# Transposes of v, decayed keys, outputs and weights moved from TensorE to VectorE's 32x32 squares and DRAM, in both mixers of a streaming encoder step

## The chip, the cores and the metric

One Trainium2 chip, one of its cores. The metric is device time in microseconds (us) of one launch, the median of three runs. TensorE (PE) does matrix products, VectorE (DVE) and ScalarE (ACT) elementwise work, GpSimd (POOL) a few small operations, SyncE (SP) issues nearly all DMAs.

## The reference, cut to what matters

One step of a two-layer encoder, on 256 prompt frames of a new stream and 32 frames of a running one, model width 1024, hidden width 2816:

```python
for l in range(2):
    x = x + 0.5 * swiglu(rms(x), ffn1)            # (silu(h @ w_gate) * (h @ w_up)) @ w_down
    x = x + (mixer_ab if l == 0 else mixer_c)(rms(x))
    x = x + 0.5 * swiglu(rms(x), ffn2)

def mixer_ab(h):                                   # 8 heads of 128 in A, 8 heads of 128 in B
    q, f, v, g, bq, bk, bv = split(h @ w_in)
    f = lb + (1 - lb) * sigmoid(f)
    # A: S_t = diag(f_t) S_{t-1} + (1 - f_t) v_t^T ;  o_t = S_t^T silu(q_t)
    o_a = rms(o) * g_out * sigmoid(g)
    # B: A[t,s] = sigmoid(z_ts) * prod_{s<j<t} (1 - sigmoid(z_tj)),  z = rms(bq) . rms(bk)
    return concat(o_a, A @ bv) @ w_out             # also returned: S, the normed bk, bv

def mixer_c(h):
    u, v = split(gelu(h @ w_in)); v = layernorm(v)
    return (u * (w_s @ v + b_s)) @ w_out           # w_s: 8 groups of 128 x 128, over positions
```

## The kernel before

Activations lie transposed, channels on the 128 partitions and 288 frames along them (32 sample frames, then 256 of the prompt). Every weight matrix is cut into chunks, of mostly 1024 rows by 256 columns, in the order in which they are used (the list `stream`). A chunk is fetched by one DMA on SP's queue, three chunks ahead (`next_chunk`, tile `wraw`), and split into a high part on ACT (`wh`, line 220) and the rest on DVE (`wl`, line 221). Each block of 128 x 128 then costs three products of 288 columns, lines 260 to 262, with the input's own two parts: 48 for a chunk of eight block rows. These are called the mains below. Two PSUM pairs named `acc` take the results of chunks in turn, four single buffers take everything else.

Mixer A/B handles the heads in four pairs. For each pair seven chunks run, f, q, v, g, bv, bk and bq (`GROUPS`). DVE's evacuation (lines 317, 318) scales each result by the norm's reciprocal. When v is there, the generator `hgrn` starts: it transposes v through DRAM (`to_rows`: DVE transposes 32 x 32 squares, four DMAs on SP put the squares in their places, one DMA reads the rows back as `vt`), runs seven levels of decay products (lines 596 to 617: A, Z, the QK rows, E and f), each with a score product on PE (line 623) whose result DVE puts in place (COPY_PREDICATED, line 633), then transposes the decayed keys on PE (line 142, `kt<-tmp`), makes the state S (696) and the outputs o (712 to 718), normalises them on ACT by squares (720), a power on POOL and a scaled copy (731), transposes them back on PE (158 and 160, `oT`) and gates them. For B, `stick_keys` and `stick` normalise bk and bq, make the stick-breaking weights (833 to 867), transpose them on PE (872 `wTs`, 883 `wT`) and multiply by values (891 to 901, `ob`). Mixer C runs eight chunks of v and eight of u, transposes each v on PE (988, `vt`), takes means of it (997), and after the eighth v normalises all of it (1038) and mixes positions (1063, 1082, `sp`). The last norm's blocks leave through `result`: six by DVE's squares and SP, two by PE transposes `y` (1330).

The generators stand in lanes: `tick`, after each block row of a chunk, gives every lane credit by its rate, and a lane with one credit takes a step to its next `yield`. The rates of the two A/B lanes are RATES, that of mixer C's is C_RATE. This is the order in which the code is written. A scheduler then settles the order on each engine, and within one engine the instructions run in that settled order, each when its semaphores allow.

Of the kernel before, what the change touches and what calls it, by code (L numbers as in the profile page):

```python
# [93 lines left out]
class Net:  # L94
    PIECE = 2
    NORM_RATE = 0.17
    RATES = (0.65, 0.55)

    def __init__(self, tc, ctx, I, O):
# [8 lines left out]
        self.rows = e(tc.tile_pool(name="rows", bufs=2, space=bass.MemoryType.DRAM))  # L108
# [287 lines left out]
    def resid(self, j, b, acc, scale, gnext):  # L396
# [4 lines left out]
        if scale == 1.0:  # L401
            nc.vector.tensor_tensor(out=x, in0=acc[b][:, :NT], in1=x, op=ALU.add)  # L402
        else:
            nc.vector.scalar_tensor_tensor(out=x, in0=acc[b][:, :NT], scalar=scale, in1=x,  # L404
                                           op0=ALU.mult, op1=ALU.add)
# [128 lines left out]
    def hgrn(self, p, pool, d):  # L534
# [146 lines left out]
        kts = []  # L681
        for b in range(2):
# [3 lines left out]
            if b == 0:  # L686
                for h in range(2):
                    r = slice(TS * h, TS * h + TS)
                    nc.scalar.copy(out=ktz[r, h], in_=pk[r, TP:TP + P])
            kts.append(kt)  # L690
            yield
        for b in range(2):
            kt = kts[b]
            pn = self.ps("S")
            for w, (x, y) in enumerate(((kt[:, 0], vw(b)[:, 0]), (kt[:, 1], vw(b)[:, 1]), (ktz[:, b], vs))):
# [9 lines left out]
        g = d["g"]  # L705
        nc.scalar.activation(out=g, in_=g, func=AF.Sigmoid)
# [20 lines left out]
        yield  # L727
        for b in range(2):
            on = T("on", [P, 384])
            for w in range(3 - b):  # L730
                nc.scalar.activation(out=on[:, w * P:w * P + P], in_=po[b][:, w * P:w * P + P], func=AF.Copy,
                                     scale=rs[:, 3 * b + w:3 * b + w + 1])
            yield
            pt = self.to_cols("oT", b, on[:, :TP].rearrange("p (w c) -> p w c", c=P), on[:, TP:])
            parts = [(b, slice(TS, NT), pt[:, :TP])]
            if b == 0:
# [645 lines left out]
```

## Time and profile before

| | us |
|---|---|
| median of 3 runs (1324.56 to 1324.66) | 1324.58 |
| the profiled execution | 1324.58 |
| its span in the trace | 1322.9 |
| PE busy | 1317.1 (100%) |
| DVE busy | 887.1 (67%) |
| ACT busy | 661.7 (50%) |
| POOL busy | 41.7 (3%) |
| DMA of the busiest queue, share of 16 engines | 53.5% |

Busy means that an instruction of the engine was at work. Matmuls overlap their neighbours in the pipeline, so what one costs is read from start to start, not from its own duration. Between the span and the profiled execution's time lie 1.7 us at the two ends. Mixer A/B runs from 260 to about 500 us of the span, each of its first three whole pairs in 61.3 to 61.4 us; mixer C from 940 to 1065 us.

### The profile page before, as it was taken

What the parts mean: (1) busy time and instruction counts of PE and PEld (TensorE: products, weight loads), DVE (VectorE), ACT (ScalarE), POOL (GpSimd) and SP (SyncE); (2) the same over time, 40 slices, a digit from 0 to 9 for tenths busy, and PEclk for the clock granted to TensorE, in tenths of its full rate; (3) what the DMA queues carried; (4) which work ended last, traced back from release to release, by engine and by line L of the source; (5) the groups of instructions that cost most, each with busy time, mean ns of one, the idle gap of its engine ahead of it and who ended that gap; (6) DMA issues with size and microseconds to landing.
All of it is one profiled execution on the core that took longest, in us unless ns stands there. A gap on an engine that the chain in (4) does not pass through costs nothing.

```text
span 1322.9 us, 24562 instructions
## 1 busy us (share of the span) xinstructions
PE 1317.1 (100%) x9922; PEld 1310.3 (99%) x9922; DVE 887.1 (67%) x1706; ACT 661.7 (50%) x1355; POOL 41.7 (3%) x70
## 2 busy tenths in 40 slices
PE   9999999999999999999999999999999999999998
PEld 9999999999999999999999999999999999999998
DVE  7666556889898866666655756655567976666653
ACT  7544445464746465544444644444655446444432
POOL 1000000010101000000000000030000000000000
PEclk9999999999999999999999999999999999999999
DMA  9555455565565546555545555576544545555453
GB/s 283 178 176 168 150 175 173 157 182 159 168 170 170 140 134 200 161 178 166 157 153 174 165 179 165 161 183 188 169 152 138 167 147 160 173 166 171 152 152 84
DMA packets 254852, 219.83 MB, mean 166 GB/s; under 512 B 41233, under 2 KB 254018, under 8 KB 254738
## 3 DMA queue, kind: packets, MB, share of 16 engines
q1 hardware_dynamic: 253906, 216.32, 53.5%
q0 software_dynamic: 672, 1.77, 0.7%
q8 instruction: 78, 1.28, 0.4%
q10 hardware_dynamic: 160, 0.17, 0.1%
q14 instruction: 36, 0.29, 0.1%
HBM read 210.89 MB, written 7.34 MB: 165 GB/s over the span
## 4 chain that ended last, share of the span: by engine, by line
PE 97%; DVE 2%; ACT 0%; issue 0%; POOL 0%; DVEq 0%
PE acc L262 30%; PE acc L261 30%; PE acc L260 30%; PE sc L623 1%; DVE wl L221 1%; PE sp L1082 1%; PE S L696 0%; PE zs L833 0%; PE acc L1157 0%; PE sc L651 0%; PE ob L900 0%; PE vt L988 0%; PE acc L280 0%; PE z L845 0%; PE ob L895 0%
## 5 line engine op out<-in xcount | busy, mean ns | idle before, releaser
L220 ACT CAST wh<-wraw 128x512 fp32r<-128x512 f32 x768 | 440.5, 619 | 490.3 <-PE acc L262 370.1
L221 DVE TENSOR_TENSOR wl<-wraw,wh 128x512 fp32r<-128x512 f32 x768 | 507.4, 688 | 253.4 <-ACT wh L220 252.9
L260 PE MATMUL acc<-xh,wl 128*128 128x288 f32 x2096 | 627.2, 299 | 0.0
L261 PE MATMUL acc<-xl,wh 128*128 128x288 f32 x2096 | 619.4, 295 | 0.0
L262 PE MATMUL acc<-xh,wh 128*128 128x288 f32 x2096 | 618.9, 295 | 0.0
L261 PEld LDWEIGHTS acc<-xl,wh 128*128 128x128 f32 x2096 | 394.1, 188 | 0.6
L260 PEld LDWEIGHTS acc<-xh,wl 128*128 128x128 f32 x2096 | 393.9, 188 | 0.4
L262 PEld LDWEIGHTS acc<-xh,wh 128*128 128x128 f32 x2096 | 393.6, 188 | 0.2
L260 PE MATMUL acc<-hh,wl 128*128 128x288 f32 x960 | 284.5, 297 | 0.0
L261 PE MATMUL acc<-hl,wh 128*128 128x288 f32 x960 | 283.4, 295 | 0.0
L262 PE MATMUL acc<-hh,wh 128*128 128x288 f32 x960 | 282.8, 295 | 0.0
L260 PEld LDWEIGHTS acc<-hh,wl 128*128 128x128 f32 x960 | 180.2, 188 | 0.8 <-DVE xT L402 0.2
L261 PEld LDWEIGHTS acc<-hl,wh 128*128 128x128 f32 x960 | 180.3, 188 | 0.1
L262 PEld LDWEIGHTS acc<-hh,wh 128*128 128x128 f32 x960 | 180.3, 188 | 0.0
L309 DVE TENSOR_TENSOR u<-acc,rb 128x576 f32<-128x576 f32 x52 | 39.3, 757 | 48.8 <-PE acc L262 48.8
L309 DVE TENSOR_TENSOR g<-acc,rb 128x576 f32<-128x576 f32 x47 | 35.6, 757 | 47.0 <-PE acc L262 47.0
L329 ACT CAST hh<-u 128x576 fp32r<-128x576 f32 x52 | 35.1, 675 | 58.4 <-DVE u L455 40.3
L330 DVE TENSOR_TENSOR hl<-u,hh 128x576 fp32r<-128x576 f32 x52 | 39.4, 758 | 7.1 <-ACT hh L329 1.3
L336 ACT ACTIVATE xh<-xT,cols 128x288 fp32r<-128x288 f32 x40 | 21.2, 531 | 24.8 <-DVE xT L404 15.4
L455 DVE TENSOR_TENSOR u<-u,g 128x576 f32<-128x576 f32 x44 | 33.1, 752 | 0.0
L453 ACT ACTIVATE g<-g 128x576 f32<-128x576 f32 x44 | 30.0, 682 | 0.1
L404 DVE SCALAR_TENSOR_TENSOR xT<-acc,xT 128x288 f32<-128x288 f32 x32 | 14.5, 455 | 17.0 <-PE acc L262 17.0
(303 smaller groups left out, 759.1 us busy)
## 6 DMA issues: line engine op xcount, KB each, us to landing
wraw<-in_ffn_w_up_dram SPq DMA_DIRECT2D x44, 1024.0 KB, 5.9
wraw<-in_ffn_w_gate_dram SPq DMA_DIRECT2D x43, 1024.0 KB, 5.4
wraw<-in_ffn_w_down_dram SPq DMA_DIRECT2D x32, 1024.0 KB, 5.7
wraw<-in_ab_w_in_dram SPq DMA_DIRECT2D x28, 1024.0 KB, 5.0
wraw<-in_c_w_in_dram SPq DMA_DIRECT2D x16, 1024.0 KB, 5.5
wraw<-in_ffn_w_down_dram SPq DMA_DIRECT2D x16, 768.0 KB, 4.6
wraw<-in_c_w_out_dram SPq DMA_DIRECT2D x8, 1024.0 KB, 5.6
wraw<-in_ab_w_out_dram SPq DMA_DIRECT2D x8, 768.0 KB, 5.2
```

Source lines behind the costliest of these rows:

```text
L220: self.nc.scalar.copy(out=h[:, x], in_=w[:, a:b])
L221: self.nc.vector.tensor_tensor(out=l[:, x], in0=w[:, a:b], in1=h[:, x].bitcast(F32), op=ALU.subtract)
L260: mm(o, lhsT=l[:, k, c], rhs=hi[:, r], start=st, stop=False)
L261: mm(o, lhsT=h[:, k, c], rhs=lo[:, r], start=False, stop=False)
L262: mm(o, lhsT=h[:, k, c], rhs=hi[:, r], start=False, stop=en)
L309: self.nc.vector.tensor_tensor(out=x, in0=acc[:, :, :NT], in1=self.rb, op=ALU.mult)
L329: nc.scalar.copy(out=hh, in_=h)
L330: nc.vector.tensor_tensor(out=self.hl[:, k:k + 2], in0=h, in1=hh.bitcast(F32), op=ALU.subtract)
L336: nc.scalar.activation(out=self.xh[:, k], in_=x, func=AF.Copy, scale=g)
L404: nc.vector.scalar_tensor_tensor(out=x, in0=acc[b][:, :NT], scalar=scale, in1=x, op0=ALU.mult, op1=ALU.add)
L453: nc.scalar.activation(out=g, in_=g, func=AF.Silu)
L455: nc.vector.tensor_tensor(out=u, in0=u, in1=g, op=ALU.mult)
```

## The change

In mixer A/B, per pair of heads: `kt` and `ktz` (decayed keys), four of the five output transposes and the two `wT` groups no longer come from PE. DVE transposes 32 x 32 squares into a tile, four DMAs on SP write them to a DRAM row tile, and one DMA (for `ktz` two more) reads them back. Seven empty steps stand between a transfer and its use. The four scalings of f by the lower bounds move from DVE to ACT. The sigmoid of g moves ahead of S. RATES go from 0.65 and 0.55 to 0.85 and 0.62, and the DRAM row tiles from 2 buffers to 6. In mixer C each v is transposed the same way in a lane of its own with rate 1.0, and means are taken one step later. The first norm's means and squares of a row stand one step ahead of its splits. At the end block 6 leaves by DVE's squares, four of its DMAs from ACT's queue, and block 7 is added up in two halves and leaves by three DMAs. Line numbers after the change are some 2 to 9 higher.

```diff
-    RATES = (0.65, 0.55)
+    RATES = (0.85, 0.62)
-        self.rows = e(tc.tile_pool(name="rows", bufs=2, space=bass.MemoryType.DRAM))
+        self.rows = e(tc.tile_pool(name="rows", bufs=6, space=bass.MemoryType.DRAM))
...
+            cuts = (0, TS + P, NT) if gnext is None and k == KD - 1 else (0, NT)
+            for a, e in zip(cuts, cuts[1:]):
+                nc.vector.scalar_tensor_tensor(out=x[:, a:e], in0=acc[b][:, a:e], scalar=scale, in1=x[:, a:e],
+                                               op0=ALU.mult, op1=ALU.add)
...
-                nc.vector.tensor_scalar(out=x, in0=x, scalar1=self.lbc[:, h:h + 1],
-                                        scalar2=self.lb[:, h:h + 1], op0=mul, op1=ALU.add)
+                nc.scalar.activation(out=x, in_=x, func=AF.Identity, scale=self.lbc[:, h:h + 1],
+                                     bias=self.lb[:, h:h + 1])
...
-            pk = self.to_tok(kd, b, "kt")
-            kt = T("kt", [P, 2, P], 2)
-            nc.scalar.copy(out=kt, in_=pk[:, :TP].rearrange("p (w c) -> p w c", c=P))
...
+        kt = T("kt", [P, 4, P])
+        rows = self.to_rows(T("QK", [P, S2 + N2], 2)[:, 0:N2], [(0, kd)])
+        nc.sync.dma_start(out=kt, in_=rows[S2:].rearrange("(i t) c -> t i c", t=P))
+        for h in range(2):
+            r = slice(TS * h, TS * h + TS)
+            nc.sync.dma_start(out=ktz[r, h], in_=rows[r])
+        g = d["g"]
+        nc.scalar.activation(out=g, in_=g, func=AF.Sigmoid)
+        for _ in range(7):
+            yield
...
-            pt = self.to_cols("oT", b, on[:, :TP].rearrange("p (w c) -> p w c", c=P), on[:, TP:])
...
+        nc.scalar.activation(out=os, in_=po[0][:, TP:384], func=AF.Copy, scale=rs[:, 2:3])
+        rows = self.to_rows(T("QK", [P, S2 + N2], 2)[:, 0:4 * P], [(0, on)])
+        ot = T("vt", [P, 5, P])
+        nc.sync.dma_start(out=ot[:, 0:4], in_=rows.rearrange("(i c) t -> c i t", c=P))
+        yield
+        pt = self.ps("oT")
+        nc.tensor.transpose(pt[:, 0:P], os, self.ident)
...
+        for _ in range(7):
+            yield
+        for h in range(2):
+            gated(h, slice(TS, NT), ot[:, 2 * h:2 * h + 2].rearrange("p w t -> p (w t)"))
...
-                nc.tensor.transpose(pw[:, i * P:i * P + P], B[b][:, i * P:i * P + P], self.ident)
...
+        for b in range(2):
+            wT = T(("wT", "pk")[b], ([P, 384], [P, 2, PAST])[b])
+            wT = wT if b == 0 else wT.rearrange("p h s -> p (h s)")[:, 0:384]
+            rows = self.to_rows(y[:, 384 * b:384 * b + 384], [(0, B[b])])
+            nc.sync.dma_start(out=wT.rearrange("p (i t) -> p i t", t=P), in_=rows.rearrange("(i s) t -> s i t", s=P))
...
-            lane = Lane(self.C_RATE)
-            self.lanes = [lane]
+            fast, lane = self.lanes = [Lane(1.0), Lane(self.C_RATE)]
...
-                        nc.tensor.transpose(pv[:, a:a + P], v[:, b, s:e], self.ident)
-                nc.scalar.copy(out=vt[:, :, n * 256:n * 256 + 256], in_=pv.rearrange("p (w c) -> p w c", w=2))
+                rows = self.to_rows(y, [(TP * b, v[:, b, TS:]) for b in range(2)])
+                for b in range(2):
+                    c = n * 256 + b * P
+                    nc.sync.dma_start(out=vt[:, :, c:c + P],
+                                      in_=rows[TP * b:TP * b + TP].rearrange("(w t) c -> t w c", t=P))
...
+            nc.vector.bn_stats(part[:n, w], xs[w][:n, 0:512])
+            nc.scalar.activation(out=junk[:n], in_=xs[w][:n, 512:D], func=AF.Square, scale=D ** -0.5,
+                                 accum_out=sa[:n, w:w + 1])
             next(split)
...
-        if k < KD - 2:
+        if k < KD - 1:
...
+                eng = nc.scalar if k == KD - 2 and a == 0 else nc.sync
...
+        for w, copy in ((0, nc.scalar.copy), (2, nc.vector.tensor_copy), (1, nc.vector.tensor_copy)):
+            n, c = ROWS[w], slice(w * P, w * P + P)
+            copy(out=y[:n, c], in_=po[:n, c])
+            to = O[1][0, :, cs] if w == 2 else O[0][0, w * P:w * P + P, cs]
+            (nc.scalar if w == 2 else nc.sync).dma_start(out=to, in_=y[:n, c])
```

What stands in a row on an engine, at three places. The first is TensorE around the score products of a middle pair of heads in mixer A/B. Before, `sc` are the scores of successive levels, and acc_4492 and acc_4587 the pair's bv and bk chunks:

```order
L262 MATMUL acc_4492<-xh,wh_4440 128x288
L623 MATMUL sc_4581<-QK_4524 128x128 x2
L260 MATMUL acc_4587<-xh,wl_4502 128x288
...
L262 MATMUL acc_4587<-xh,wh_4501 128x288
L623 MATMUL sc_4622<-QK_4558 128x128 x2
L626 MATMUL sc_4622<-QK_4558 128x128
L260 MATMUL acc_4587<-xh,wl_4502 128x288
...
L262 MATMUL acc_4587<-xh,wh_4542 128x288
L623 MATMUL sc_4657<-QK_4602 128x128 x2
L628 MATMUL sc_4657<-QK_4602 128x64
L260 MATMUL acc_4587<-xh,wl_4543 128x288
```

Before, 18 mains stand between one score and the next. After, with acc_4719 the pair's bq chunk and acc_4844 the next pair's f chunk:

```order
L262 MATMUL acc_4719<-xh,wh_4682 128x288
L625 MATMUL sc_4531<-QK_4474 128x128 x2
L628 MATMUL sc_4531<-QK_4474 128x128
L909 MATMUL ob_4535<-pk_4335,bvt_3937 128x256
L625 MATMUL sc_4565<-QK_4514 128x128 x2
L625 MATMUL sc_4600<-QK_4550 128x128 x2
...
L625 MATMUL sc_4661<-QK_4612 128x128 x2
L625 MATMUL sc_4692<-QK_4647 128x128 x2
L142 MATMUL kt_4792<-ident,bk_4716 128x128 x2
L144 MATMUL kt_4792<-ident,bk_4716 128x128
L142 MATMUL kt_4809<-ident,bk_4716 128x128 x2
L260 MATMUL acc_4844<-xh,wl_4729 128x288
```

After, six scores, an `ob` product and the three groups that transpose bk (`kt<-ident,bk`) follow each other with no main between them; the first main behind them reads wl_4729.

The second place is VectorE over the same stretch. Before, `bq_4813` is the evacuation of the bq chunk (acc_4686); wl_4696 and wl_4771 are the two halves of the next pair's f chunk, wl_4826 the first half of its q chunk:

```order
L221 TENSOR_TENSOR wl_4696<-wraw_4493,wh_4695 128x512
...
L221 TENSOR_TENSOR wl_4771<-wraw_4493,wh_4770 128x512
L617 TENSOR_TENSOR f_4141<-f_4141 128x4x64
L221 TENSOR_TENSOR wl_4771<-wraw_4493,wh_4770 128x512
L673 TENSOR_TENSOR qz_2519<-q_4261,f_4141 128x2x32
L674 TENSOR_TENSOR q_4261<-q_4261,f_4141 128x256
L676 TENSOR_TENSOR tmp_4797<-k_4391,E_4398 128x320
L677 TENSOR_TENSOR tmp_4797<-k_4391,E_4398 128x2x128
L781 TENSOR_SCALAR ks_4756<-kms_4755 128x5
L221 TENSOR_TENSOR wl_4826<-wraw_4588,wh_4825 128x512
L317 TENSOR_TENSOR bq_4813<-acc_4686,rb_2579 128x2x2x128
```

Before, all of the f chunk's splits stand ahead of the evacuation. After, `bq_4841` is the evacuation, and wl_4729 the first half of the next pair's f chunk:

```order
L221 TENSOR_TENSOR wl_4683<-wraw_4386,wh_4682 128x512 x2
...
L618 TENSOR_TENSOR E_4418<-E_4418,f_4170 128x144x2
L317 TENSOR_TENSOR bq_4841<-acc_4719,rb_2579 128x2x2x128
L619 TENSOR_TENSOR f_4170<-f_4170 128x144x2
L598 TENSOR_TENSOR QK_4514<-k_4411,E_4418 128x40x4
...
L635 COPY_PREDICATED sc_4443<-lv,sc_4531 128x128x2
...
L676 TENSOR_TENSOR q_4276<-q_4276,f_4170 128x256
L679 TENSOR_TENSOR tmp_4713<-k_4411,E_4418 128x2x128
L221 TENSOR_TENSOR wl_4729<-wraw_4500,wh_4728 128x512
L168 STREAM_TRANSPOSE QK_4735<-tmp_4713 128x576
L221 TENSOR_TENSOR wl_4729<-wraw_4500,wh_4728 128x512
```

After, 41 rows of the levels and their end (left out in part) stand between the evacuation of bq and the first split for the next chunk; before, the levels' end stood ahead of the evacuation.

The third place is VectorE in mixer C, where v gives way to u. Before, wl_11528 and wl_11569 are the halves of the second u chunk (acc_11612), and v_11437 and v_11514 the evacuations of the last two v chunks:

```order
L221 TENSOR_TENSOR wl_11485<-wraw_11291,wh_11484 128x512 x2
L221 TENSOR_TENSOR wl_11528<-wraw_11367,wh_11527 128x512 x2
L309 TENSOR_TENSOR v_11437<-acc_11366,rb_10949 128x576
L221 TENSOR_TENSOR wl_11569<-wraw_11367,wh_11568 128x512 x2
L309 TENSOR_TENSOR v_11514<-acc_11441,rb_10949 128x576
L997 BN_STATS st_10885<-vt_10882 128x6 x2
```

After, u_11667 and u_11770 are the evacuations of the first and second u chunk (acc_11591, acc_11681); wl_11601 and wl_11644 are the halves of the second, wl_11691 the first half of the third (acc_11773):

```order
L168 STREAM_TRANSPOSE lnb_11525<-v_11508 128x256 x2
L309 TENSOR_TENSOR u_11667<-acc_11591,rb_10977 128x576
L221 TENSOR_TENSOR wl_11601<-wraw_11433,wh_11600 128x512 x2
L221 TENSOR_TENSOR wl_11644<-wraw_11433,wh_11643 128x512 x2
L168 STREAM_TRANSPOSE vo_11604<-v_11587 128x256 x2
L309 TENSOR_TENSOR u_11770<-acc_11681,rb_10977 128x576
L221 TENSOR_TENSOR wl_11691<-wraw_11513,wh_11690 128x512
```

Before, a chunk's first split stood ahead of the evacuations of the chunks that run two and three places before it. After, it stands right behind the evacuation of the chunk that runs just before it.

## Rows read from the trace of the kernel before

**Rows 1.** The page: busy times, granted clock in 40 slices, chain of waits.

```profile
PE 1317.1 (100%) x9922; PEld 1310.3 (99%) x9922; DVE 887.1 (67%) x1706; ACT 661.7 (50%) x1355; POOL 41.7 (3%) x70
...
PEclk9999999999999999999999999999999999999999
...
PE 97%; DVE 2%; ACT 0%; issue 0%; POOL 0%; DVEq 0%
```

**Rows 2.** TensorE's waits: total us, times, longest; the five there are, first and last.

```profile
PE acc L1157 <- DVE ms L1168: 1.2, 1, 1.2
...
PE kn L158 <- DVE bkt L786: 0.2, 1, 0.2
```

**Rows 3.** Windows: window, length, busy us (instructions) PE, PEld, DVE, ACT, POOL, clock, DMA.

```profile
24.00:200.00 176.00, 176.00 (x1330) 176.00 (x1329) 109.64 (x181) 84.03 (x146) 0.00 (x0) 1.00 0.55 173
```

**Rows 4.** Timeline of TensorE, three key transposes between mains: start us, length us.

```profile
334.22 0.30 PE L262 MATMUL acc<-xh,wh 128*128 128x288 f32 x1
334.35 0.38 PE L142 MATMUL kt<-ident,tmp 128*128 128x128 f32 x2
...
334.82 0.30 PE L261 MATMUL acc<-xl,wh 128*128 128x288 f32 x1
```

**Rows 5.** Timeline of VectorE, one level of decay products with its placement.

```profile
376.03 0.32 DVE L596 TENSOR_TENSOR QK<-k,E 128x160 f32<-128x160 f32 x1
376.26 0.29 DVE L597 TENSOR_TENSOR QK<-k,E 128x128 f32<-128x128 f32 x1
...
377.27 0.73 DVE L633 COPY_PREDICATED sc<-lv,sc 128x256 f32<-128x256 uint8 x1
377.79 0.50 DVE L617 TENSOR_TENSOR f<-f 128x288 f32<-128x288 f32 x1
378.20 0.32 DVE L596 TENSOR_TENSOR QK<-k,E 128x160 f32<-128x160 f32 x1
```

**Rows 6.** Groups of VectorE, 306.27 to 490.30 us: busy us, mean ns, idle before.

```profile
L221 DVE TENSOR_TENSOR wl<-wraw,wh 128x512 fp32r<-128x512 f32 x83 | 55.5, 688 | 5.7 <-ACT wh L220 5.4
L639 DVE COPY_PREDICATED SS<-ls,sc 64x64 f32<-64x64 uint8 x15 | 3.4, 224 | 0.1
L168 DVE STREAM_TRANSPOSE kn<-bv 128x576 f32<-128x576 f32 x3 | 2.3, 762 | 0.0
L317 DVE TENSOR_TENSOR bq<-acc,rb 128x512 f32<-128x512 f32 x3 | 2.0, 678 | 0.0
```

**Rows 7.** Timeline of TensorE, one score (three products in it) between mains.

```profile
375.77 0.30 PE L262 MATMUL acc<-xh,wh 128*128 128x288 f32 x1
375.91 0.61 PE L623 MATMUL sc<-QK 128*128 128x128 f32 x4
...
376.71 0.30 PE L261 MATMUL acc<-xl,wh 128*128 128x288 f32 x1
```

**Rows 8.** Groups of ScalarE and GpSimd, 306.27 to 490.30 us, in the normalisation.

```profile
L731 ACT ACTIVATE on<-o,pw 128x128 f32<-128x128 f32 x15 | 4.6, 374 | 0.1
...
L720 ACT ACTIVATE on<-o 128x128 f32<-128x128 f32 x15 | 4.1, 275 | 7.7 <-PE o L718 6.8 <-PE o L714 0.6
...
L720 ACT ACTIVATION_READ_ACCUMULATOR on<-o 128x1 f32 x15 | 2.9, 194 | 0.0
...
L134 POOL TENSOR_TENSOR pw<-oms,mhalf 128x5 f32<-128x5 f32 x3 | 3.8, 1256 | 34.0 <-DVE oms L724 34.0
```

**Rows 9.** A window of mixer C, where positions are mixed; columns as in rows 3.

```profile
1020.00:1030.00 10.00, 10.00 (x80) 10.00 (x80) 10.00 (x23) 4.84 (x9) 0.00 (x0) 1.00 0.44 126
```

**Rows 10.** DMA issues: queue, operation, count, KB of each, median us to landing.

```profile
rows<-QK SPq DMA_DIRECT2D x16, 80.0 KB, 2.1
vt<-rows SPq DMA_DIRECT2D x4, 320.0 KB, 4.6
```

**Rows 11.** Timeline of the end: the last sum and the last copy before the output.

```profile
1318.37 0.46 DVE L404 SCALAR_TENSOR_TENSOR xT<-acc,xT 128x288 f32<-128x288 f32 x1 [1.95 <-PE acc L262]
...
1319.46 0.37 ACT L1332 COPY sq<-y 128x256 f32<-128x256 f32 x1 [0.40 <-PE y L1330]
```

More of the change, by code (lines that the diff above doesn't have):

```diff
@@ L680, in hgrn @@
         Sn = T("Sn", [P, 2, 2, P])
-        kts = []
-        for b in range(2):
-            pk = self.to_tok(kd, b, "kt")
-            kt = T("kt", [P, 2, P], 2)
-            nc.scalar.copy(out=kt, in_=pk[:, :TP].rearrange("p (w c) -> p w c", c=P))
[L686 to L690, printed above, removed]
+        kt = T("kt", [P, 4, P])
[7 more added lines that the diff above has]
+        for _ in range(7):
             yield
         for b in range(2):
-            kt = kts[b]
             pn = self.ps("S")
-            for w, (x, y) in enumerate(((kt[:, 0], vw(b)[:, 0]), (kt[:, 1], vw(b)[:, 1]), (ktz[:, b], vs))):
+            for w, (x, y) in enumerate(((kt[:, b], vw(b)[:, 0]), (kt[:, 2 + b], vw(b)[:, 1]), (ktz[:, b], vs))):
                 mm(pn[:, w * P:w * P + P], lhsT=x, rhs=y, start=True, stop=True)
@@ L878, in store @@
             nc.vector.tensor_tensor(out=self.hl[:, k, t], in0=x, in1=self.hh[:, k, t].bitcast(F32), op=ALU.subtract)
-        def turned(b):
-            pw = self.ps("wT")
-            for i in range(3):
-                nc.tensor.transpose(pw[:, i * P:i * P + P], B[b][:, i * P:i * P + P], self.ident)
-            wT = T("wT", [P, 384])
-            nc.scalar.copy(out=wT, in_=pw[:, :384])
-            return wT
-        wT = turned(0)
+        wTs = []
+        y = T("kn", [P, 2 * (PAST + NT)])
+        for b in range(2):
[3 more added lines that the diff above has]
+            nc.sync.dma_start(out=wT.rearrange("p (i t) -> p i t", t=P), in_=rows.rearrange("(i s) t -> s i t", s=P))
+            wTs.append(wT)
         yield
@@ L896, in stick @@
         store(slice(kk, kk + 2), slice(0, TS), po[:, 0:S2].rearrange("p (h t) -> p h t", h=2))
-        yield
+        for _ in range(7):
+            yield
         for b in range(2):
             po = self.ps("ob")
+            wT = wTs[b]
             mm(po[:, 0:256], lhsT=vt[:, 1 + b], rhs=wT[:, 0:256], start=True, stop=False)
             mm(po[:, 128:256], lhsT=vt[:, 3 + b], rhs=wT[:, 256:384], start=False, stop=True)
-            if b == 0:
-                wT = turned(1)
             store(kk + b, slice(TS, NT), po[:, :TP])
@@ L995, in tokens @@
                     nc.scalar.copy(out=vs[:, j], in_=pv[:, :P])
-                    for w in range(2):
-                        nc.vector.bn_stats(st[:, w, j], vt[:, w, (n - 1) * 256:(n + 1) * 256])
-                    yield
+                elif n:
+                    means(n // 2 - 1)
+                yield
             spw = spatial_weights()
@@ L1018, in statistics @@
                 mv = state["mv"] = T("mv", [P, 3, 2])
+                means(J - 1)
                 sp = T("sp", [P, 6])
@@ L1042, in sample_out @@
             def sample_out():
[L1044 removed]
+                gb, bb, y = (T(n, [P, J * P]).rearrange("p (j c) -> p j c", c=P) for n in ("lng", "lnb", "vo"))
                 for to, name in ((gb, "c_ln_g"), (bb, "c_ln_b")):
@@ L1239, in first_block @@
                 keep(5, a)
-            nc.vector.bn_stats(part[:n, w], xs[w][:n, 0:512])
-            nc.scalar.activation(out=junk[:n], in_=xs[w][:n, 512:D], func=AF.Square, scale=D ** -0.5,
-                                 accum_out=sa[:n, w:w + 1])
         for w, n in enumerate(ROWS):
```

50 lines of the change are left out of this document (18 added, 32 removed).

## The prediction

> **What bounds the kernel now.** I read the page first. TensorE is busy for 1317.1 of the span's 1322.9 us and makes 97% of the chain of waits [rows 1]; VectorE is busy for 67% and ScalarE for 50%. The view of TensorE's waits sums to 2.3 us in five waits [rows 2]. So the time is TensorE's own instructions in a row, and an edit gains what it takes from that row and loses what it makes TensorE wait. In a window of nothing but mains, 1330 of them take 176.00 us, 0.132 us each [rows 3]. Then I read the order of the changed kernel against that of before, and asked at each place what TensorE has at hand when a row of the other engines becomes serial. Durations below are rows of before.
>
> **What TensorE is rid of.** Per pair of heads 5 transposes of keys, 4 of outputs and 6 of weights go, in four pairs 60; in mixer C 32 and at the end 3: 95 together. Three of them between two mains move the main after next from 334.22 + 0.27 to 334.82 [rows 4]: 0.60 - 0.27 = 0.33, so 0.11 us each. 95 x 0.11 = **-10.4 us**. The copies of their results on ScalarE, the scalings moved to it and the 32 x 32 transposes on VectorE (0.76 us for 576 columns [rows 6]) lie beside mains as long as TensorE has any; both engines have room, and I cost them at nothing outside the places below. A rule of the Trainium skill speaks against this part: "VectorE: DVE Perf Modes", "Rules for kernel authors", leaves a full 128 x 128 transpose to TensorE where the result may lie in PSUM, and the 32 x 32 ones to VectorE. By it this term would be 0; the rows, with TensorE full, price it at -10.4, and I take the rows.
>
> **The score bunches.** This is the largest term. Before, a score product stands between each 18 mains, and the next pair's f chunk is split on VectorE before bq is evacuated. After, in pairs 1, 2 and 3 (pair 0 keeps its spacing), six scores stand together behind the bq chunk, and VectorE has evacuation, 41 rows, and only then the first split on which the next main waits. The evacuation needs the last main of bq, so none of it can run ahead. Summed: evacuation 0.68 [rows 6]; four levels with placement at 378.20 - 376.03 = 2.17 [rows 5], 8.7; the last level without placement and sample columns, 2.17 - 0.52 - 0.2, 1.5; the first f 0.4; four placements of the sample at 0.22, 0.9 [rows 6]; the part of `hl` and the closing products qz, tmp twice and q, five of some 0.2 to 0.5, between a small and a large row of [rows 6], 1.6; the split 0.69 [rows 6]. That is 14.5; rows that follow each other overlap by some 0.1 (0.32 long, next start 0.23 later [rows 5]), where the levels' 2.17 holds this already, so I take 13.8. TensorE has in that time the scores: one with three products costs 376.71 - 375.77 - 0.27 = 0.67 [rows 7], with two of them two thirds, 0.44; three of each, 3.3. Five transposes of bk are 0.55, the `ob` product by columns (384 against 128 at 0.22) 0.7 to 0.9: 4.8. So 13.8 - 4.8 = 9.0 idle per bunch, x 3 = **+27 us**. Bounds: the levels at their rate without overlap 14.5, at a tenth less 12.4, which gives 23 to 29.
>
> **The smaller waits per pair.** From one pair's S bunch to the next score bunch I find six, three times over.
> (1) bk to bq: the evacuation and then the split of bq stand behind the last main of bk: 0.68 + 0.69 [rows 6], 1.4.
> (2) The transposes `ss` of bq take the PSUM buffer that the scaled copies (731 before) release. Behind the last o product come two squares at 0.275 + 0.194, POOL's power 1.26 and four copies at 0.374 [rows 8], with VectorE's small step 0.2 in between: 3.9 + 0.3 for the hand-overs, against 18 mains, 2.4: 1.8.
> (3) The one `oT` transpose left waits for its scaled copy, which stands on ScalarE behind three copies of kn, bq's scaling, a sigmoid, five squares and a cast: 26 mains cover 3.4 of some 5: 1.5.
> (4) `wTs` waits for the sample's scan on VectorE: 1.0. (5) Its product waits for ScalarE's copy behind eight sigmoids: 0.4.
> (6) The bv chunk's first split stands behind the placement of a score that closes the chunk before: 0.52 [rows 5] and 0.69, 1.2.
> Sum 7.3, x 3 = **+21.9**. I have (3) to (5) from rows of ScalarE and VectorE alone and take 0 and double as their ends; (1), (2) and (6) to within a third: 3 x (3 to 11.7), 9 to 35.
>
> **The end of mixer A/B.** The last pair has the same waits with less cover: `ss` 1.9, `oT` with 3 mains instead of 26 ahead of it 4.6, `wTs` 0.7. Then two `ob` products wait for the weights' way through DRAM: a write lands 2.1 after its issue, a read of rows up to 4.6 [rows 10], against some 6 us of mains and products that stand between: 3. The output chunk waits for the last `hl`, 1. **+11**, between 5 (reads of this size at 2.1) and 15.
>
> **Mixer C.** There the first split of five chunks (the first to fifth of u) now stands right behind the evacuation of the chunk ahead: 0.76 - 0.1 + 0.69 = 1.4 each, with some 0.6 for second halves behind means: 7.6. The normalisation of v comes two chunks later than before. VectorE is busy there for all of ten us [rows 9], while TensorE lives on splits made ahead. After, that lead is gone: behind the evacuation of the fourth u chunk TensorE waits for POOL's power and the first normalised columns (2.3), and the sixth's first split stands behind the rest of the normalisation and one spatial step, nine scalings of 0.46 and some 4.6 of products, 9.4 with the split, while TensorE has 5 us: 4.4. Together **+14**, between 5, if half of the splits are early enough after all, and 20.
>
> **The ends.** The norm's step at the start: TensorE is fed by the weights there, 0 within 0.5. At the end the last sum of 0.46 goes in two halves and the copy of 0.37 likewise [rows 11]; a half of each leaves the path, **-0.4**, within 0.5.
>
> Sum: 1324.6 - 10.4 + 27 + 21.9 + 11 + 14 - 0.4 = 1387.7, against the profiled execution, which is the median of the runs (its span plus 1.7 us). I forecast **1388 us**, +4.8%.
>
> **The rivals.**
> The transposes alone: VectorE's row is done while TensorE has work, and 1324.6 - 10.8 = 1314 stands. For it: VectorE is only 67% busy. Its place is the score bunch, and it decides when all waits together fall under 10.8 us, 3.6 per bunch with none elsewhere, that is when the row behind bq's evacuation takes 8.4 us instead of 13.8. Against it: the level's 2.17 us are a plain row of VectorE's work without a wait in it [rows 5].
> Only the score bunches: the smaller waits and mixer C are covered, since every idle time of TensorE lets the others get ahead. 1324.6 - 10.8 + 27 = 1341. For it: those waits are each under 2 us and read from several engines' rows.
> TensorE's clock: it is granted in full in all 40 slices of before [rows 1], where TensorE never rests. In a bunch it is at work for a third of 14 us. If the clock falls there to the lower of its two levels, 1.2 of 2.4 GHz, the mains behind it take twice as long until it is back. No row of before shows how long that would be. Between nothing and one chunk, 48 x 0.132 = 6.4 us, I take 3.2 at five places (three bunches, the end of A/B, the sixth u chunk): +16, 1404. The Trainium skill has this rule, in "TensorE: Matmul & The Clock Gate", section "Part 1: The HAM clock gate": an idle array is throttled to 1.2 GHz and is given its full rate after sustained work. No row of before can show it.
> DRAM's way: the keys' or outputs' read lands after TensorE asks for it in every pair, since four writes and three reads stand on SP's queue among weight fetches. Twice 2.1 + 4.6 [rows 10] against the 60 and more mains (8 us) that stand between write and S would cost some 3 to 5 us a pair: 1400.
> That nothing is changed in effect (within 0.2%, about what a measurement of this kernel can tell) would need waits of 8 to 13 us in all.
>
> **How the numbers follow.** Forecast 0.50, clock 0.19, only the bunches 0.13, DRAM's way 0.07, transposes alone 0.09, no difference 0.02. Faster is 0.09, same 0.02, slower 0.89. The range leaves out the transposes alone and a little above the clock's case: from 1338, the bunches alone with their lower bound, to 1408.
>
> **What would show it.** In the profile after, TensorE's busy share falls to about 95%, and its waits name VectorE's split (line 221) in first place with three waits of about 9 us, at one place per pair, then ScalarE's scaled copy and line 221 again in mixer C. VectorE and ScalarE grow by little. A granted clock under 1.00 behind a bunch would show the third rival, waits on reads of rows the fourth. The prediction is wrong if the view of TensorE's waits sums to less than 20 us, or if its largest waits lie elsewhere.

## The result

The changed kernel takes 1406.62 us in the median (1403.83 to 1408.56), the kernel before 1324.57 in the same comparison: 1.0618 times as long, 95% interval 1.0599 to 1.0637. The profiled execution takes 1407.47 us with a span of 1405.8, so 82.9 us more than the 1324.58 of before. The forecast was 1388 us, with a range of 1338 to 1408.

The page of the changed kernel, its lines that answer to [rows 1]:

```profile
PE 1339.5 (95%) x9827; PEld 1321.9 (94%) x9827; DVE 897.7 (64%) x1724; ACT 655.1 (47%) x1338; POOL 45.1 (3%) x70
...
PEclk9999999998998988999999999999998899999999
...
PE 86%; DVE 7%; issue 4%; ACT 2%; POOL 1%; DMA 0%; POOLq 0%; ACTq 0%; DVEq 0%
```

95 of TensorE's instructions are gone, and yet it is busy for 22.4 us longer: the clock has holes, and a product takes longer in them. TensorE's waits, which were five and 2.3 us together [rows 2], are now 48 and 62.6 us (line and releaser: us, times, longest); the first seven:

```profile
PE acc L260 <- DVE wl L221: 27.1, 17, 3.1
PE sc L625 <- DVE QK L602: 9.4, 6, 1.9
PE ss L142 <- ACT tmp L731: 6.0, 4, 1.7
PE wTs L879 <- DVE Bsz L871: 4.1, 3, 1.5
PE acc L260 <- ACT hh L329: 3.9, 1, 3.9
PE sc L625 <- DVE SS L641: 3.7, 3, 1.2
PE sc L625 <- DVE QK L600: 2.7, 6, 0.6
```

VectorE's split (221) is in first place. No wait names a read of DRAM rows. From the start of a stage's first main to that of the next stage's, the two traces differ only here; the forecast's terms are put beside it, each less its transposes at 0.11 us:

| | before | after | difference | forecast |
|---|---|---|---|---|
| mixer A/B, input (28 chunks) | 235.30 | 282.27 | +46.97 | 27 + 21.9 - 45 x 0.11 = +43.9 |
| mixer A/B, output (8 times 48 mains, each called a chunk here) | 62.94 | 76.64 | +13.70 | 11 - 15 x 0.11 = +9.4 |
| mixer C (24 chunks) | 167.02 | 189.55 | +22.53 | 14 - 32 x 0.11 = +10.5 |
| start and end | | | -0.3 | -0.4 - 3 x 0.11 = -0.7 |

A score bunch in the timeline of TensorE of the changed kernel (start us, length us, and in brackets how long it waited and for whom), against [rows 7], where mains stood between the scores:

```profile
411.03 0.30 PE L262 MATMUL acc<-xh,wh 128*128 128x288 f32 x1
411.17 0.60 PE L625 MATMUL sc<-QK 128*128 128x128 f32 x4
...
413.25 0.71 PE L625 MATMUL sc<-QK 128*128 128x128 f32 x4 [0.60 <-DVE QK L600]
415.83 1.20 PE L625 MATMUL sc<-QK 128*128 128x128 f32 x4 [1.87 <-DVE QK L602]
...
422.67 1.20 PE L625 MATMUL sc<-QK 128*128 128x128 f32 x4 [1.24 <-DVE SS L641]
...
425.18 0.61 PE L260 MATMUL acc<-xh,wl 128*128 128x288 f32 x1 [0.25 <-DVE wl L221]
...
428.46 0.44 PE L261 MATMUL acc<-xl,wh 128*128 128x288 f32 x1
428.70 0.44 PE L262 MATMUL acc<-xh,wh 128*128 128x288 f32 x1
...
429.26 0.29 PE L262 MATMUL acc<-xh,wh 128*128 128x288 f32 x1
```

The last main of bq ends at 411.33, the next main begins at 425.18: 13.85 us. The same stretch in windows (columns as in [rows 3]):

```profile
411.00:425.00 14.00, 8.98 (x42) 7.46 (x40) 13.48 (x45) 6.28 (x18) 0.66 (x2) 0.66 0.20 40
425.00:430.00 5.00, 4.82 (x23) 4.82 (x24) 3.94 (x11) 1.76 (x9) 1.82 (x2) 0.60 0.42 74
430.00:440.00 10.00, 10.00 (x77) 10.00 (x76) 6.39 (x15) 5.03 (x10) 0.00 (x0) 1.00 0.70 191
```

VectorE is busy for 13.48 of 14 us: it is the bound there. TensorE's granted clock falls, and the mains behind the bunch are 0.44 us long and 0.24 apart until 428.9, where before they are 0.30 long and 0.133 apart. The six waits of this bunch sum only to 5.2 us, since TensorE's own products take up to twice as long in it (a score of four products 0.60 us at 411.17 and 1.20 at 415.83); that costs nothing more there, as VectorE sets the pace. So the view of waits shows less than what the bunch costs.

In mixer C the same timeline, all engines, from the first main of the second u chunk to where that chunk ends:

```profile
1065.67 0.37 PE L260 MATMUL acc<-xh,wl 128*128 128x288 f32 x1 [2.89 <-DVE wl L221]
...
1071.98 0.29 PE L262 MATMUL acc<-xh,wh 128*128 128x288 f32 x1
1072.31 0.76 DVE L309 TENSOR_TENSOR u<-acc,rb 128x576 f32<-128x576 f32 x1 [4.30 <-PE acc L262]
1073.10 0.68 ACT L1111 ACTIVATE u<-u 128x576 f32<-128x576 f32 x1 [6.74 <-DVE u L309]
1073.69 2.17 ACT L220 CAST wh<-wraw 128x512 fp32r<-128x512 f32 x4
1074.33 0.69 DVE L221 TENSOR_TENSOR wl<-wraw,wh 128x512 fp32r<-128x512 f32 x1 [1.26 <-ACT wh L220]
...
1075.16 0.58 PE L260 MATMUL acc<-xh,wl 128*128 128x288 f32 x1 [2.89 <-DVE wl L221]
```

VectorE rests 4.30 us ahead of the evacuation and ScalarE 6.74 us ahead of its Gelu, both with the next chunk's split still to do. They have the time; their order doesn't let them use it. The split then waits for a cast on ScalarE, which stands behind the Gelu of the chunk just evacuated. Such a wait of 2.89 us is there four times, one of 1.54 ahead of them.

### The profile page after: what moved, and what is told of

Read it like the earlier page. It is cut to its first block, busy times and chain, and to the rows that moved or that the text cites. A ratio compares the mean times of both kernels' runs of the same rounds, so it can differ in the third digit from the quotient of the medians.

```text
span 1405.8 us, 24612 instructions
## 1 busy us (share of the span) xinstructions
PE 1339.5 (95%) x9827; PEld 1321.9 (94%) x9827; DVE 897.7 (64%) x1724; ACT 655.1 (47%) x1338; POOL 45.1 (3%) x70
## 4 chain that ended last, share of the span: by engine, by line
PE 86%; DVE 7%; issue 4%; ACT 2%; POOL 1%; DMA 0%; POOLq 0%; ACTq 0%; DVEq 0%
PE acc L260 27%; PE acc L261 27%; PE acc L262 27%; DVE wl L221 2%; POOL pw L134 1%; ACT on L718 1%; PE acc L280 0%; DVE f L619 0%; DVE E L618 0%; DVE sc L635 0%; PE S L696 0%; PE sc L625 0%; DVE QK L600 0%; PE acc L1166 0%; DVE x L1098 0%
## 5 line engine op out<-in xcount | busy, mean ns | idle before, releaser
L260 PEld LDWEIGHTS acc<-xh,wl 128*128 128x128 f32 x2096 | 398.2, 190 | 26.6 <-issue 21.1
L261 PEld LDWEIGHTS acc<-xl,wh 128*128 128x128 f32 x2096 | 398.2, 190 | 0.6
L262 PEld LDWEIGHTS acc<-xh,wh 128*128 128x128 f32 x2096 | 397.8, 190 | 0.1
L625 PE MATMUL sc<-QK 128*128 128x128 f32 x112 | 24.1, 350 | 15.8 <-DVE QK L602 9.4
L625 PEld LDWEIGHTS sc<-QK 128*128 128x128 f32 x112 | 19.1, 239 | 19.6 <-issue 14.0
L336 ACT ACTIVATE xh<-xT,cols 128x288 fp32r<-128x288 f32 x40 | 21.3, 531 | 26.7 <-DVE xT L406 15.4
L884 ACT CAST hh<-ob 128x256 fp32r<-128x256 f32 (+1 forms) x12 | 3.8, 319 | 62.9 <-PE ob L910 55.8
```

The lines of the kernel that those rows point to most:

```text
L260: mm(o, lhsT=l[:, k, c], rhs=hi[:, r], start=st, stop=False)
L261: mm(o, lhsT=h[:, k, c], rhs=lo[:, r], start=False, stop=False)
L262: mm(o, lhsT=h[:, k, c], rhs=hi[:, r], start=False, stop=en)
L336: nc.scalar.activation(out=self.xh[:, k], in_=x, func=AF.Copy, scale=g)
L625: mm(ps[:, b * P:b * P + P], lhsT=X[:, col(0, b)], rhs=X[:, B2].rearrange("p (w h t) -> p w h t", w=2, h=2)[:, :, b], start=True, stop=True)
```

## Experiments

**The parts, each alone.** The kernel before with one part of the change, by the hunks of the diff above. First the ends:

```diff
-        if k < KD - 2:
+        if k < KD - 1:
...
+        for w, copy in ((0, nc.scalar.copy), (2, nc.vector.tensor_copy), (1, nc.vector.tensor_copy)):
```

> The kernel before with only the two ends of the change: the first norm's means one step ahead, block 6 by VectorE's squares, block 7 in halves. The prediction's term is -0.4 us within 0.5, so 1324.2 (1323.7 to 1324.7). The profile of after shows the start 0.3 us shorter (18.13 to 17.81 us to the first product of 288 columns); by that row 1324.0. If the ends carried part of the loss it would lie above 1325.

Measured: 1324.39 us, ratio 0.9999 (0.999 to 1.0008). The ends neither gain nor lose what can be measured.

Then mixer C's part, with six row buffers:

```diff
-                        nc.tensor.transpose(pv[:, a:a + P], v[:, b, s:e], self.ident)
+                rows = self.to_rows(y, [(TP * b, v[:, b, TS:]) for b in range(2)])
```

> The kernel before with only mixer C's part (and the six DRAM row buffers). Theory of the order: VectorE's first splits of the u chunks stand behind the evacuation of the chunk ahead, and TensorE waits at each; the stages of after (v +0.1, u +21.5, output +0.9) give 1324.6 + 22.5 = 1347. The prediction's own term, less its 32 transposes (3.5 us), is +14 - 3.5, so 1335. If mixer C lost only because of something left over from mixer A/B (clock, queues), it would be near 1321.

Measured: 1347.07 us, ratio 1.0169 (1.0155 to 1.0183).

Then mixer A/B's part:

```diff
-    RATES = (0.65, 0.55)
+    RATES = (0.85, 0.62)
...
+        rows = self.to_rows(T("QK", [P, S2 + N2], 2)[:, 0:N2], [(0, kd)])
...
+        rows = self.to_rows(T("QK", [P, S2 + N2], 2)[:, 0:4 * P], [(0, on)])
...
+            rows = self.to_rows(y[:, 384 * b:384 * b + 384], [(0, B[b])])
```

> The kernel before with only mixer A/B's part (rates, rows' buffers, scalings, keys, outputs and weights by squares and DRAM). Theory of the order: the three score bunches and the waits around them are all there, so +47.0 + 13.7 us as in the stages of after: 1385. If the parts of A/B and C hinder each other (shared buffers and queues), this run and the one of mixer C alone sum to clearly less than after's +82; if they are independent, the three runs of this call sum to it within 3 us.

Measured: 1384.89 us, ratio 1.0457 (1.0443 to 1.0472). The three differences, -0.2, +22.5 and +60.3, sum to 82.6; the whole change has +82.05. The parts don't hinder each other, and each keeps its waits by itself.

**The order on the one queue.** In the settled order of SP's queue of the changed kernel, fetches of weights stand behind row writes that wait for VectorE. SP's queue in mixer C, in the timeline and in the view of its waits:

```profile
1061.86 1.95 SPq L172 DMA_DIRECT2D rows<-lnb  x4
1063.85 0.51 SPq L193 DMA_DIRECT2D wraw<-in_c_w_in_dram  x1
```

```profile
SPq L172 <- DVE lnb L168: 16.2, 4, 7.7
```

The four writes are issued when VectorE's transposes of v have ended (1061.83), and the fetch behind them. This kernel is the changed one with:

```diff
-            self.nc.sync.dma_start(out=w[:, k:k + n], in_=ap.rearrange("(k p) c -> p k c", p=P))
+            with self.tc.high_priority():
+                self.nc.sync.dma_start(out=w[:, k:k + n], in_=ap.rearrange("(k p) c -> p k c", p=P))
```

> The changed kernel whole, with one difference: the weight fetches on SP's queue are given precedence when the order is settled, so that they don't stand behind the row transfers there. The same instructions, the same transposes, writes and reads of rows. Theory of the order (the splits stand late because the fetches stand behind row writes that wait for VectorE): in the settled order the three score bunches and mixer C's five late splits are gone, one late group is left at A/B's output chunk; so 1314 + 5 to 30 us: 1319 to 1344. Rival (the way through DRAM, or VectorE's and ScalarE's added work itself, starves TensorE): 1390 or more, as after.

Measured: 1492.9 us, ratio 1.1275 (1.1258 to 1.1293), 86 us slower than the change. The theory of the order missed; the number lies with the rival's "1390 or more", but far above the "as after" that it stood for. Timelines of TensorE, then of SP, in its last pair:

```profile
575.65 0.63 PE L142 MATMUL kt<-ident,bk 128*128 128x128 f32 x2
590.69 1.19 PE L697 MATMUL S<-vt,kt 128*128 128x128 f32 x4 [14.41 <-issue]
```

```profile
577.19 0.85 SPq L172 DMA_DIRECT2D rows<-QK  x2
581.77 0.39 SPq L194 DMA_DIRECT2D wraw<-in_ab_w_out_dram  x1
582.20 1.08 SPq L172 DMA_DIRECT2D rows<-QK  x2
...
587.68 0.38 SPq L686 DMA_DIRECT2D kt<-rows  x1
```

Of the keys' four writes two are issued; then a weight fetch stands in the queue, issued at 581.77, and only behind it the other two writes and at 587.68 the read. A fetch waits for its buffer, which VectorE's splits release (SP's longest such wait is 18.4 us). The queue issues in its order, and a transfer behind a waiting one waits too. What was missing in my theory is that the row transfers suffer as well as the fetches. What the other stages lose here wasn't taken apart.

**Row transfers on a queue of their own.** The changed kernel with every write and read of rows issued by GpSimd, nine lines of this kind:

```diff
-            nc.sync.dma_start(out=to[q], in_=y[TS * q:TS * q + TS].rearrange("t (n c) -> t n c", c=TS))
+            nc.gpsimd.dma_start(out=to[q], in_=y[TS * q:TS * q + TS].rearrange("t (n c) -> t n c", c=TS))
```

> The changed kernel whole, but all writes and reads of DRAM rows are issued from GpSimd's queue, so that on SP's queue the weight fetches stand among themselves as in the kernel before, and neither kind waits behind the other (with the fetches given precedence on the one queue, the run before this showed the reverse fault: the row transfers stood behind fetches and landed up to 19 us late). Theory of the shared queue: in the settled order the score bunches' late splits and mixer C's five are gone, one late group of 114 rows is left at A/B's output chunk; the transposes' gain of 10.8 us shows less that one group and some waits of 1 to 3 us per pair: 1319 to 1349. Rival (the added work of VectorE and ScalarE in series, or the way through DRAM itself, starves TensorE whichever queue it takes): 1370 or more, with waits on reads of rows or the same first splits.

Measured: 1391.25 us, ratio 1.0502 (1.0485 to 1.0518). The total lies with the rival, and in A/B's output so do the waits on reads of rows; the other stages lie with the theory. A/B's input loses +16.4 where it lost +47.0, the three bq chunks -1.4, +1.4 and +3.5 where each had +12.7, and mixer C's u stage +0.9 where it had +21.5; waits on line 221 fall from 27.1 us in 17 to 1.6 in two:

```profile
PE S L696 <- DMA ktz<-rows: 13.2, 2, 12.4
PE ob L909 <- DMA wT<-rows: 3.5, 3, 2.2
PE acc L260 <- DVE wl L221: 1.6, 2, 1.0
```

So with the queue parted the late splits and their waits are gone, with every transpose still by squares and DRAM. What eats most of the gain is new, and in one place: the third chunk of 48 mains of A/B's output takes 56.3 us instead of 9.45. There the last pair's transfers stand in series; the issues on GpSimd, and the product that waits for them on TensorE:

```profile
503.98 2.67 POOL L172 DMA_DIRECT2D rows<-QK  x4 [12.37 <-DVE QK L168]
...
511.79 0.77 POOL L685 DMA_DIRECT2D kt<-rows  x1 [3.82 <-DMA rows<-QK]
...
515.24 1.19 PE L696 MATMUL S<-vt,kt 128*128 128x128 f32 x4 [12.44 <-DMA ktz<-rows]
```

From the first write's issue to the product lie 11.3 us, and no mains are left to cover them. The Trainium skill, in "DMA: Bandwidth & Descriptors", section "Issuing engines are not separate DMA queues", says that issuing from several engines saves only the time to initiate a DMA. That speaks of the transfers; here another issuer took 20.6 us from mixer C's u stage, since with it the late splits are gone from the order.

In the next kernel the last pair's keys, outputs and weights come from TensorE again, as in the kernel before, and most of the empty steps ahead of their use go with the transfers:

```diff
+        last = p == 3
+        if not last:
...
+                pk = self.to_tok(kd, b, "kt")
...
+                    nc.tensor.transpose(pt[:, w * P:w * P + P], on[:, c:c + P], self.ident)
...
+                    nc.tensor.transpose(pw[:, i * P:i * P + P], B[b][:, i * P:i * P + P], self.ident)
```

> The changed kernel with the row transfers on GpSimd's queue, and the last pair of heads alone with its keys, outputs and weights transposed on TensorE as in the kernel before (so 80 of the 95 transposes are gone). With the transfers on that queue one output chunk of mixer A/B took 56.3 us: there the last pair's ways through DRAM stand one behind the other with few products of the weights left to cover them (the keys from the first write's issue at 503.98 to the state product at 515.24, the weights from 540.20 to 548.65 and on to 551.6). Theory of ways in series: without them this chunk is some 20 to 25 us shorter, 1366 to 1371. Rival (the 112 rows of VectorE that stand ahead of that chunk's splits are the price, whatever the way): over 1380.

Measured: 1371.36 us, ratio 1.0354 (1.0339 to 1.0368), 0.4 us above what ways in series gave, and well under the rival's 1380. That output chunk falls from 56.3 to 34.9 us. The series, with its empty steps, was 21 us of it; what the rest of A/B's +47 us here is made of (the longest waits are `oT` for ScalarE, 7.3 us in four, and first products for evacuations of g, 6.1 in two) I haven't tried.

**Mixer C's missed term.** The kernel with mixer C's part alone, less ScalarE's Gelu of u, which is left out:

```diff
-                nc.scalar.activation(out=u, in_=u, func=AF.Gelu_apprx_tanh)
+                pass
```

> The kernel before with mixer C's part alone, as in the second run, and without the Gelu of u on ScalarE (its work is left out: u goes on as it was evacuated). The settled order of TensorE's and VectorE's late splits is the same. In mixer C TensorE waits 2.89 us at each of four first splits, where the prediction had 1.4; in the trace ScalarE's Gelu of the chunk just evacuated (0.68 us) stands ahead of the cast on which the split waits. Theory (the missed term is ScalarE's Gelu in the row): each of four or five waits falls by 0.6 to 0.7, so 1347.1 - 2.6 to 3.4 = 1344, a little less if the clock is up sooner. Rival (the wait is VectorE's evacuation and splits alone): 1347 within 1.

Measured: 1336.2 us, ratio 1.0088 (1.0075 to 1.0102), 10.9 us faster than with it, three times what I expected. The same place in this kernel:

```profile
1011.07 1.14 ACT L220 CAST wh<-wraw 128x512 fp32r<-128x512 f32 x2 [0.23 <-PE acc L262]
1011.07 0.76 DVE L309 TENSOR_TENSOR u<-acc,rb 128x576 f32<-128x576 f32 x1 [4.31 <-PE acc L262]
...
1012.57 0.37 PE L260 MATMUL acc<-xh,wl 128*128 128x288 f32 x1 [1.54 <-DVE wl L221]
```

and one window of each, with the Gelu and without:

```profile
1015.00:1025.00 10.00, 8.13 (x48) 7.93 (x48) 4.38 (x7) 1.82 (x4) 0.00 (x0) 0.83 0.42 130
```

```profile
1015.00:1025.00 10.00, 8.46 (x64) 8.25 (x63) 3.58 (x6) 2.96 (x6) 0.00 (x0) 1.00 0.54 152
```

TensorE's waits on line 221 in the u stage, with the Gelu and without:

```profile
PE acc L260 <- DVE wl L221: 13.1, 5, 2.9
```

```profile
PE acc L260 <- DVE wl L221: 7.9, 6, 1.5
```

The cast now runs beside the evacuation, and the wait is 1.54 us. These waits fall from 13.1 to 7.9 us, 5.2 of the 10.9. Most of the rest is the clock: it stays at 1.00 in all of mixer C, and mains recorded as longer than 0.38 us in mixer C fall from 56 to 11 (45 x 0.107 = 4.8; counted by the granted clock, 51 mains start at its lower level with the Gelu and none without, 5.5). So one missed step of ScalarE had doubled the wait, and the longer wait also brought the clock down.

**The clock in the bunches.** The changed kernel with six products that nothing reads ahead of each later score in pairs 1 to 3:

```diff
+            for _ in range(6 if p and i else 0):
+                mm(ps[:, :NT], lhsT=self.onr, rhs=self.xh[:, 0], start=True, stop=True)
```

> The changed kernel whole, with six products of 288 columns that nothing reads (0.8 us at the full clock) ahead of each score of a later level, in pairs 1 to 3, so that TensorE rests less inside the bunches; the settled order keeps the same late groups. It measures the clock's share of the loss: if the clock is the main price there, the mains behind a bunch run at the full clock again and it is some 9 us (three bunches of 3 us) faster than after: 1395 to 1400. If the clock falls all the same or the added products only fill idle time, it is level with after, 1404 to 1409; if they stand in the way, slower.

Measured: 1414.46 us, ratio 1.0677 (1.0663 to 1.0692). Inconclusive on the clock: the added products run in lumps, and the clock falls all the same, only later. TensorE in the same bunch:

```profile
420.70 3.18 PE L625 MATMUL sc<-xh,onr 128*128 128x288 f32 x12
...
431.23 0.44 PE L260 MATMUL acc<-xh,wl 128*128 128x288 f32 x1
```

Twelve stand in one row. Of its mains 141 are longer than 0.38 us, of the changed kernel's 139, so the clock's price wasn't taken away, and the products only stood in the way.

**Versions that keep only a part.** The kernel before with A's outputs alone, on SP's queue:

```diff
+        rows = self.to_rows(T("QK", [P, S2 + N2], 2)[:, 0:4 * P], [(0, on)])
+        ot = T("vt", [P, 5, P])
+        nc.sync.dma_start(out=ot[:, 0:4], in_=rows.rearrange("(i c) t -> c i t", c=P))
```

> The kernel before with one part of the change alone: mixer A's outputs by VectorE's squares and DRAM (16 of the 95 transposes; row buffers 6), on SP's queue. No first split stands late in its settled order. Theory: the part gains its transposes, 16 x 0.11 = 1.8 us, where the order stays: 1322.8. Rival (each way through DRAM costs TensorE a wait per pair, 1 to 4 us): 1327 to 1339.

Measured: 1327.48 us, ratio 1.0024 (1.0015 to 1.0033). No bunch, no late split, and the part still loses 2.9 us, 2.5 of it in A/B's output: its waits are small (`kt` for VectorE 1.3 us, `zs` for ScalarE 0.9, `ob` for a copy 0.6) and spread.

A's outputs, mixer C's part and the ends, with the rows on GpSimd's queue (in this kernel and the next two the reads of the cached keys, eight per pair, are issued there as well):

```diff
+        nc.gpsimd.dma_start(out=ot[:, 0:4], in_=rows.rearrange("(i c) t -> c i t", c=P))
...
+                    nc.gpsimd.dma_start(out=vt[:, :, c:c + P],
```

> The kernel before with A's outputs, mixer C's part and the two ends of the change, the row transfers all on GpSimd's queue. No first split stands late in its settled order. Theory of the shared queue: 48 transposes and the ends are gained, 1324.6 - 5.3 - 0.2 = 1319.1, and mixer C's u stage falls from 79.3 to about 58 us. Rival (VectorE's own row in mixer C, busy for all of ten us around the normalisation, starves TensorE in any order): u stage 65 us or more, 1327 or more.

Measured: 1328.41 us, ratio 1.003 (1.0019 to 1.0042). The total misses the theory's 1319.1 by 9.3 us and lies with the rival's number. The u stage is 58.9 us, as the theory of the queue has it, against 79.3 with the rows on SP. But mixer C in all comes to +0.87 where its transposes give -3.5: v -1.56, u +0.91, output +1.52. A/B loses 3.0 where its outputs give -1.8.

Mixer C's part for the first six v and the ends, on that queue, the last two v on TensorE:

```diff
+                if n < 6:
+                    y = T(("lnb", "vo")[n % 2], [P, 2 * TP])
...
+                else:
+                    yield
+                    pv = self.ps("vt")
```

> The kernel before with mixer C's part for the first six v chunks alone (the last two are transposed on TensorE as before), row transfers on GpSimd's queue, and the two ends of the change. Theory: mixer C's u stage loses only where the last v's way makes the normalisation late; with the last two on TensorE, 24 transposes are gained, 24 x 0.11 = 2.6 us, and the ends' 0.2: 1321.8. Rival (the normalisation's place isn't it; small waits of VectorE's added squares and of GpSimd's transfers take the gain back, as with all eight, where stage C came to +0.9 instead of -3.5): 1324 to 1326.

Measured: 1323.47 us, ratio 0.9993 (0.9984 to 1.0002), between theory and rival. Mixer C comes to -0.83 (v -1.07, u +0.92, output -0.68), so the last v's way is part of what was lost, but not all. Too little to be told from no change.

The same, and B's weights of the first three pairs:

```diff
+            if p < 3:
+                rows = self.to_rows(y[:, 384 * b:384 * b + 384], [(0, B[b])])
```

> The run before last (mixer C's first six v, the ends, row transfers on GpSimd's queue; 1323.5 us) with one part of mixer A/B's change added: B's weights by VectorE's squares and DRAM in the first three pairs of heads, the last pair on TensorE as in the kernel before. Another 18 transposes are gone. No first split stands late in the settled order. Theory (a part gains its transposes where the order stays and a following pair covers its way through DRAM): 18 x 0.11 = 2.0 us, 1321.5, faster than the kernel before by 0.2%. Rival (in mixer A/B each way through DRAM costs small waits of its own, as the outputs alone did: +2.9 where -1.8 was expected): 1324 to 1328.

Measured: 1333.73 us, ratio 1.0071 (1.0057 to 1.0084); a miss. In the profiled execution (1331.03 us) A/B's input loses 6.3 us; TensorE's first waits, and a wait of VectorE:

```profile
PE sc L625 <- DVE QK L600: 2.9, 2, 2.6
PE kn L158 <- DVE bkt L788: 2.8, 3, 0.9
PE sc L628 <- POOL QK L604: 1.4, 2, 0.9
```

```profile
DVE QK L598 <- DMA rows<-QK: 2.7, 2, 2.5
```

GpSimd's own copies (604) now stand behind row transfers in its queue, and VectorE waits for a buffer that such a write still reads. So this queue has its waits too. None of the versions beats the kernel before by what can be measured.

## Why the prediction was right, and what it missed

**Bound and direction: right.** TensorE was full, and an edit loses what it makes TensorE wait. The transposes' -10.4 us were not measured by themselves; the second and third v chunk of mixer C are shorter by 0.67 and 0.43 us, where four transposes each are gone, 0.17 and 0.11 apiece.

**The score bunches: right to within 0.1 us each.** The chain was forecast at 13.8 us and runs 13.85; less the forecast's own 4.8 for TensorE's work that is 9.05, forecast 9.0, and the three bq chunks are alike within 0.01 us. I said that the waits would show as three of 9 us; they show as six in each bunch.

**The smaller waits: near in sum, wrong in two.** In the pair whose bunch is shown (348 to 425 us) the trace has bk to bq 1.60 (forecast 1.4), `ss` 1.41 (1.8), `wTs` 1.38 (1.0) and the bv chunk's split 1.34 (1.2). The waits for `oT` (1.5) and the sample's weights (0.4) are not there. That is 5.7 against 7.3. The pair takes 77.17 us where it took 61.37, +15.8; bunch and waits less 15 transposes give 13.1, and 10 mains at the lower clock (348.0 to 350.5) 1.1; 1.6 us stays spread out.

**The end of mixer A/B: too low by 4.4.** Waits of 1.73 (`ss`), 3.15 (a first split), 3.94 and 0.32 (the output's parts, forecast 1) and 0.46 sum to 9.6; the terms for `oT` (4.6), `wTs` (0.7) and DRAM (3) didn't come, and the first split wasn't forecast, so that the sum is near by luck. Together with 18 slow mains, 1.9 us (22, 2.4 us, counted by the granted clock), that is 11.5 to 12 of the 15.4 us lost before the transposes are taken off; the windows there have clocks of 0.73 and 0.66, which stretch the other products too, and I haven't measured them apart.

**Mixer C: the step that failed.** I put evacuation and split at 1.4 us, as if the high part's cast were at hand. I had not looked at ScalarE's row at this place, where the Gelu stands ahead of the cast: 2.89 us. Without the Gelu the wait is 1.54 and mixer C comes to +11.6 us, forecast +10.5. So the term was mis-sized by one step of ScalarE and by the clock that it brought down. That +11.6 is so near +10.5 is luck in part: the last two terms of the sum, 2.3 for POOL's power and 4.4 at the sixth chunk, came to 2.20 and 0.64 us (the mixing products, `sp`) and 0.15 without the Gelu, and to 1.91 and 0.15 in the changed kernel.

**The clock: the third rival happened as well.** I kept it apart from the forecast as an alternative; it was an addition. Mains longer than 0.38 us, which are 45 before (records that run together) and 139 after, count 16 more in A/B's input, 18 more in its output and 60 more in mixer C: 94 x 0.107 = 10.1 us, where the rival had 16 at five places. That count is low, since fewer records run together after than before: while the granted clock is at its lower level 112 mains start (26, 22 and 64), 12.0 us. Most of them stand in mixer C, at the places that I had undersized. 1387.7 + 10.1, plus 4 x 1.5 us for the Gelu, is 1403.8, 3.7 short of the profiled execution (1.8 by the second count). Errors the other way stand in that sum too (1.6 us in the smaller waits of the pair looked at, 4.6 in mixer C's last two terms), so that its nearness is luck in part. So is it that the measured time lies in the range: its upper end came from this rival's guess of 16 us, set beside the forecast and not on top of it. Its lower end is 1.2 us off its own terms, 1324.6 - 10.8 + 23 = 1336.8.

**The other rivals.** The way through DRAM was not waited for in the changed kernel. It shows once the queue's order changes, in waits of up to 14.4 us with the fetches first and 12.4 us with the rows on GpSimd. That only the bunches cost, or nothing but the transposes' gain counts, falls with the +22.5 us of mixer C and the +13.7 of A/B's output.

**Where the order comes from.** That the shared queue is the condition of the late splits is shown: parted, they vanish from order and trace. That the scheduler reckons weights to land late because fetches stand behind row writes is argued only; in the trace they don't land late, as no wait of VectorE on line 221 names a fetch, and ScalarE's cast (220) waits for one once in the whole run, for 1.2 us, in an FFN.

## What to carry to other kernels

Before work is moved off a full engine, read in the new order what stands between an evacuation and the next chunk's first operand on every engine of that chain, ScalarE's too; a wait forgotten there can count once in itself and again in the clock. Keep transfers that wait for computed data and prefetches that wait for buffers on different queues, and look at what else stands in the second queue. Take the clock as something that comes on top of waits, not as a case beside them.

## What was not expected of the hardware

Waits far shorter than the bunches brought TensorE's clock to the lower of its two levels. In mixer C it stays at 1.00 with one wait of 1.54 us at each of the first five u chunks (Gelu left out); with 2.89 us it falls, though not behind each: in the changed kernel the main at 1065.67 us, behind the same 2.89 us, is 0.37 us long, the one at 1075.16 is 0.58. A wait of 2.20 us of the mixing products (`sp`) comes with a falling clock in the run of mixer C's part (1050.56 us) and with the full one where the Gelu is left out (1041.61). In the bunch shown it falls between 413.25, where a score of four products is 0.71 us long, and 415.83, where it is 1.20, and it is back 3.7 us after the next main (425.18 to 428.9). The Trainium skill, in "TensorE: Matmul & The Clock Gate", section "Part 1: The HAM clock gate", has the throttle of an idle array and the return after sustained work; the trace agrees, with 0.24 us between mains at the lower level and 0.133 at the full one.
